# States and output products put in front of the attention scores, with a shorter opening: a one-core decoder layer on Trainium2

## The chip, the cores and the metric

The kernel runs on one core of a Trainium2 chip. The metric is the device time of one execution in microseconds (us). Before the change it was 455.96 us, the median of 3 runs (455.81 to 457.31). The profiler recorded one execution by itself, of 455.39 us; its trace spans 453.6 us, and all times of the trace count from the start of that span. The engines are called PE (matrix products), PEld (PE's weight loads), DVE (vector), ACT (scalar functions), POOL and SP; SP's work here is to issue DMA transfers.

## What is computed

One decoder layer over 512 tokens of width 1024. The input is normalised and multiplied with one wide weight matrix, whose columns are cut into branches:

```python
aq, ak, av, ag, bq, bf, bi, bg, gate_a, gate_b = jnp.split(proj, split_pts, axis=-1)
# attention branch: 8 heads of 64
qa = rmsnorm(heads(aq), q_norm_gain[i])
ka = rmsnorm(heads(ak), k_norm_gain[i])
ya = moba_attention(qa, ka, va, rel_bias)          # logits + bias, softmax, times values
ya = (ya * silu(ag)) @ w_up_a[i]
# recurrent branch: 4 heads of 128
log_f = log_sigmoid(fpre) + log1p(lb * exp(minimum(-fpre, EXP_CLIP)))
kb = (1.0 - lb) * sigmoid(-fpre);  qb = silu(bq);  vb = bi
yb = hgrn2_chunkwise(qb, kb, vb, log_f)            # chunk by chunk:
#   out   = (q * exp(cum)) @ state + scores @ v
#   state = state * exp(last) + (k * exp(last - cum)).T @ v
yb = (rmsnorm(yb, hgrn_out_gain) * silu(bg)) @ w_up_b[i]
merged = sigmoid(gate_a) * ya + sigmoid(gate_b) * yb
h = h + merged @ w_out[i];  h = h + (p @ w_ple) * sigmoid(h @ w_ple_gate)
```

All is in float32. Every large product is split into three: each operand is a rounded high half and a low half, and high·high, high·low and low·high are added up.

## The kernel before, in words

A projection is 24 products of 128x128 by 128x512: 8 slices of the inner dimension, three products each (`mm3`, L282). The weight slices come in by DMA as `wf`; ACT makes the high half `wh` (L217), DVE the low half `wl` (L218). The projections run in this order: `bi`, `av` (values), `bf0`, `bq0`, `aq`, `ak`, then the table `ORDER` (`bg0`, `ag0`, `bf1`, ...), then the up-projections, the output and the last gate. The two letters name the branch of the weight, `ga`/`gb` the merge gates, and the digit the head or the column block.

Into this stream of dense products small ones are woven. The recurrent branch works head by head (h = 0 to 3): the gates (`hgrn_gates`), the products within a chunk `lpb` and `lpa` (`hgrn_intra`, tiles of 128x32), the chunk states (`hds` products, then `st` on DVE), and the output products `hop` (`hgrn_out`). The attention branch works pair of heads by pair of heads: the scores `s` of step 0 (query blocks 0 to 2) and of step 1 (block 3), the softmax, sixteen SP transfers per step that turn the probabilities (L836), and the products with the values, `o`. `s01` is written here for head pair 0, step 1.

PE's order is fixed as the program writes it. A planner (`tick`, `run_due`, `spawn`) decides where: it adds up the expected time of the dense products, and a generator that is due puts its products there. `PACE` is the planner's time between two attention steps. The output products `hop` of a head wait in a list `hops` until the next head's `hgrn_intra` comes to `lpb`; `hds` follows `lpa` of its own head at once. The order on ACT, DVE and SP is made by a scheduler from costs and due times; `held` makes an instruction stand behind the last dense product written so far, `in_order` and `tc.high_priority` set rank.

PSUM, where the products land, is a set of banks: three for the pool `mm` (projections, `hop`, `o` and the third score tile `s{hp}0x`), two for `g` (`lpb`, `lpa`, `hds`), three for `a` (`aq`, `ak`, the other score tiles). A product that starts a new tile waits until the last reader of the bank's former tile is done. For a gate projection (`bg1`, `bg2`, ...) that reader is the DVE multiply at the end of `silu_block` (L479), behind three ACT instructions (exp, ln, exp); for a `bq` it is the multiply at L514.

At the start, nine products of ones (`warm`, L184) run on PE while the first data comes: `xhead` (L328), then the first weight's first slice in two transfers of 256 columns (L330), all on SP's queue; the small constants `smalls` come by ACT's queue (L179). `lower_bound` (L205 to L213) computes a few 128x4 constants from them.

Of the kernel before, what the change touches and what calls it, by code (L numbers as in the profile page):

```python
# [28 lines left out]
LEVELS = (16, 8, 4, 2, 1)  # L29

STEPS = ((0, 1, 2), (3,))
PACE = (21.0, 21.0)

HP = 2.5
H0 = 8.0
# [8 lines left out]

EARLY = (2, 3, 4, 5)

WARM = 9

XN = (0.6,) * 7 + (2.0, 0.6)

# [13 lines left out]
def hybrid_layer_kernel(  # L64
# [75 lines left out]

    dense = []

    def held(inst):

        tc.add_manual_dep(inst.ins, dense[-1].ins.name,
                          mybir.DependencyInfo(mybir.DependencyClass.NoSync, mybir.DependencyReason.SCHED_ONLY))
        return inst

    def held_from(us, insts, until=None):

        def later():
            for inst in insts if until not in done else []:
                held(inst)
            yield 0.0

        spawn(later(), us)
# [19 lines left out]
    raw0 = unit("w", "wf0", shape=(128, 2, 512))  # L176
    A.preload_act_table_set("natural_log_exp_and_others")
    with tc.high_priority():
        nc.scalar.dma_start(sm, smalls)  # L179

    warm = bank("g", "warm")
# [20 lines left out]
    lbv, ln1mlb = lb[:, 3], lb[:, 5]  # L202

    def lower_bound():
        V.tensor_scalar(qgain, sm[:, 8:9], 0.125, None, op0=OP.mult)  # L205
        V.tensor_copy(lb[:, 0], lbl)
        V.tensor_sub(lb[:, 1], lbl, lb[:, 0])
        A.activation(lb[:, 1], lb[:, 1], AF.Exp)
        V.reciprocal(lb[:, 2], lb[:, 1])
        V.tensor_mul(lb[:, 2], lb[:, 1], lb[:, 2])  # L210
        V.tensor_sub(lb[:, 3], lb[:, 2], lb[:, 2])
        V.tensor_scalar(lb[:, 4], lb[:, 3], -1.0, 1.0, op0=OP.mult, op1=OP.add)
        A.activation(lb[:, 5], lb[:, 4], AF.Ln)  # L213


    def split(hi, lo, src):
        A.activation(hi, src, AF.Copy)  # L217
        V.tensor_tensor(lo, src, hi.bitcast(F32), op=OP.subtract)  # L218
# [2 lines left out]
        A.activation(hi, src, AF.Copy, scale=g)  # L221
        V.scalar_tensor_tensor(lo, src, g, hi.bitcast(F32), op0=OP.mult, op1=OP.subtract)

    wseq, wraw, wtile, wpos = [], [], [], [0]
    late = []

    def w_sequence():
# [31 lines left out]
    def w_split(upto):  # L259
        while len(wtile) <= min(upto, len(wseq) - 1):  # L260
            i = len(wtile)
            w_load(i)
            ap, kn, cols = wseq[i]
            hi = unit("wh", f"wh{i}", R, (128, kn, cols))
            lo = unit("wl", f"wl{i}", R, (128, kn, cols))
            split(hi, lo, wraw[i])
            wtile.append((hi, lo))

    def weight(ap, ahead=LD):
# [56 lines left out]

    with tc.high_priority():
        nc.sync.dma_start(xfirst, xhead)  # L328
        for i in range(2):
            nc.sync.dma_start(raw0[:, 0, 256 * i:256 * i + 256], wseq[0][0][:, 0, 256 * i:256 * i + 256])  # L330
        x0 = unit("H", "xr0")
        xr.append(x0)
        nc.sync.dma_start(x0[:, 256:512], xT[0][:, 256:512])
        raw1 = unit("w", "wf1", shape=(128, 2, 512))
        wraw.append(raw1)
        nc.sync.dma_start(raw1[:, 0], wseq[1][0][:, 0])
        load_x(1, 2)
        nc.sync.dma_start(raw0[:, 1], wseq[0][0][:, 1])
        nc.sync.dma_start(raw1[:, 1], wseq[1][0][:, 1])
        load_x(2, 3)  # L340
# [141 lines left out]


    hg = {}
    hops = []

    runs = [1000]

# [28 lines left out]
    def hgrn_intra(h):  # L517
# [50 lines left out]
        k16 = kq(16)  # L568
        yield HP
        yield from beside_attention()  # L570
        while hops:
            hops.pop()()
        lpb = bank("g", f"lpb{h}").rearrange("p (l c t) -> p l c t", l=4, c=NT)
        big = lpb[:, 2:4].rearrange("p l c t -> p (l c t)").rearrange("p (c t) -> p c t", c=NT)
        lpa = bank("g", f"lpa{h}").rearrange("p (l c t) -> p l c t", l=4, c=NT)
# [50 lines left out]
        if not h:  # L626
# [4 lines left out]
        V.tensor_tensor(q[:, 128:], q[:, 128:], cum[:, 128:], op=OP.mult)  # L631
        turned = A.activation(kd[:, :nk].rearrange("p (c g k) -> p g c k", c=3, g=4),
                              kts[:, :nk].rearrange("p (g c k) -> p g c k", g=4, c=3), AF.Copy)
        held(turned) if h == 0 else held_from(2.0, [turned], f"hds{h}")
        yield from beside_attention()
        for i, k_ in enumerate(ks):
            diag(lpa[:, 1 + i], k_, k_, LEVELS[1 + i])
# [4 lines left out]
            A.activation(sc[s_, :, s_], s32[s_], AF.Copy)  # L642
        hg[h] += (kd,)

    def hgrn_out(h, vb, sbg):
        kb, q, cum, kd = hg[h][:4]
        hv = slice(h * 128, h * 128 + 128)
        dsp = bank("g", f"hds{h}")
        done.add(f"hds{h}")
        for c in range(3):  # L650
            PE.matmul(dsp[:, c * 128:c * 128 + 128], kd[:, c * 128:c * 128 + 128], vb[c][:, hv],
                      start=True, stop=True)
        cost(0.65)
        st = unit("st", f"st{h}", shape=(128, 3, 128))
        V.tensor_copy(st[:, 0], dsp[:, 0:128])
        for c in (1, 2):
            e = c * 128 + 127
            V.scalar_tensor_tensor(st[:, c], st[:, c - 1], cum[:, e:e + 1], dsp[:, c * 128:c * 128 + 128],
                                   op0=OP.mult, op1=OP.add)
        op_ = []  # L660

        def products():
            op_.append(bank("mm", f"hop{h}"))
            for c in range(NT):
                s_ = slice(c * 128, c * 128 + 128)
                PE.matmul(op_[0][:, s_], vb[c][:, hv], sc[:, c, :], start=True, stop=(c == 0))
                if c:
                    PE.matmul(op_[0][:, s_], st[:, c - 1], q[:, s_], start=False, stop=True)
            cost(1.5)

        if h < GH - 1:
            hops.append(products)
            yield lambda: op_
        else:
            yield HOP
            products()
        op_ = op_[0]
        o = unit("YB", f"ho{h}")
        y = unit("N", f"hy{h}")
        A.activation(o, op_, AF.Square)  # L680
        gated = f"bg{h}" in done
        if gated:
            V.scalar_tensor_tensor(sbg[h], op_, ogain[:, h:h + 1], sbg[h], op0=OP.mult, op1=OP.mult)
        token_spread(y, token_factor(token_sums(o, y, 1.0 / 128)))
        if gated:
            V.tensor_tensor(sbg[h], sbg[h], y, op=OP.mult)
        else:
            V.scalar_tensor_tensor(o, op_, ogain[:, h:h + 1], y, op0=OP.mult, op1=OP.mult)
        hg[h] += (None if gated else o,)
# [28 lines left out]
    def qk_norm(name, banks, g, res):  # L718
# [6 lines left out]
        for t in range(NT):  # L725
            raw = pb[:, (0 if name == "q" else 4) + t]
            with tc.high_priority(offset=AHEAD):
                A.activation(raw, banks[t], AF.Copy)
            sq = pb[:, 8 + t % 2]
            A.activation(sq, raw, AF.Square)  # L730
            V.tensor_reduce(ss[:, t], sq.rearrange("p (h d) -> p h d", h=HEADS), axis=AX.X, op=OP.add)
            raws.append(raw)
        V.tensor_scalar(ss, ss, 1.0 / 64, None, op0=OP.mult)
        rsqrt(y, t_, ss)
        for t in range(NT):
# [38 lines left out]
    def attention(qn, kn, va, sags, res):  # L774
# [92 lines left out]
        for n in range(len(steps) + 1):  # L867
            if n >= 1:
                yield PACE[steps[n - 1][1]]
            if n < len(steps):  # L870
                hp, i = steps[n]
                if i == 0:
                    for j in range(2):
                        t = unit("T", f"bias{hp}{j}")
                        row = ed[2 * hp + j:2 * hp + j + 1, :]
                        held(nc.sync.dma_start(t, bass.AP(tensor=row.tensor, offset=row.offset,
                                                          ap=[[1, 128], [1, 512]])))
                        T[hp, j] = t
                where = scores(hp, i)
            if n >= 1 and steps[n - 1][1] == NS - 1:  # L880
                ho = steps[n - 1][0]
# [256 lines left out]
```

## Time and profile before

| | before |
|---|---|
| time, median of 3 (lowest to highest) | 455.96 us (455.81 to 457.31) |
| profiled execution, its span | 455.39 us, 453.6 us |
| PE busy | 448.7 us, 99% |
| DVE, ACT busy | 303.1 us, 276.5 us |
| granted PE clock | 0.999 |
| POOL's DMA queue, SP's DMA queue, share of 16 engines | 22.7%, 20.0% |

How it is read: the timeline gives start, duration, engine, source line, operation, output <- inputs, and in brackets how long the engine sat idle before it and what ended that. A PE product's recorded duration (0.39 us for 512 columns) is longer than the distance to the next one's start (0.227 us), because products overlap; costs on PE are therefore taken from start to start. "PEld" rows are the weight loads. "issue" means that the profile shows no event that was waited for.

### The profile page before, as it was taken

How to read it: one execution, taken by the hardware profiler on the slowest of the kernel's cores; microseconds unless marked ns; L12 is line 12 of the kernel's file. 1: busy time of each engine (PE TensorE's matmuls, PEld its weight loads, DVE VectorE, ACT ScalarE, POOL GpSimd, SP SyncE). 2: the span in 40 equal slices, each digit the busy share in tenths (PEclk: the TensorE clock that was granted, in tenths of full speed). 3: DMA queues.
4: the chain of work that ended last, by engine and by line, in shares of the span. 5: the costliest groups of instructions: out<-in, count | busy, mean ns of one | idle time of the engine just before them, and what ended most of it. 6: DMA issues, size and time to landing. Idle time of an engine off the chain costs nothing.

```text
span 453.6 us, 8108 instructions
## 1 busy us (share of the span) xinstructions
PE 448.7 (99%) x3066; PEld 372.3 (82%) x3066; DVE 303.1 (67%) x616; ACT 276.5 (61%) x532; POOL 38.4 (8%) x77
## 2 busy tenths in 40 slices
PE   9999999999999999999999999999999999999996
PEld 8888888788888888878888888878888888888886
DVE  5869493876898795959985866454479744544322
ACT  5957574737679986979887987683334433222201
POOL 1000100000000000010101000101220100000000
PEclk9999999999999999999999999999999999999999
DMA  8802433258492527162526352545731644230111
GB/s 257 322 1 95 139 104 117 79 201 185 166 260 74 171 53 220 30 177 92 163 86 175 103 160 95 166 143 139 249 94 48 229 141 140 92 115 25 46 48 46
DMA packets 31846, 59.49 MB, mean 131 GB/s; under 512 B 6976, under 2 KB 16960, under 8 KB 31808
## 3 DMA queue, kind: packets, MB, share of 16 engines
q0 software_dynamic: 9056, 32.51, 22.7%
q1 hardware_dynamic: 22608, 26.47, 20.0%
q8 instruction: 24, 0.39, 0.4%
q14 instruction: 14, 0.11, 0.1%
q10 hardware_dynamic: 144, 0.01, 0.0%
HBM read 48.74 MB, written 4.98 MB: 118 GB/s over the span
## 4 chain that ended last, share of the span: by engine, by line
PE 81%; DVE 7%; SPq 4%; DMA 3%; ACT 2%; issue 2%; DVEq 0%; ACTq 0%
PE g L282 10%; PE ga L282 10%; PE h L282 10%; PE ub L282 5%; PE ua L282 5%; PE av L412 5%; PE bi L412 5%; PE aq L412 4%; SPq L836 4%; PE ak L412 4%; PE gb L282 4%; PE bf L282 4%; PE ag L282 4%; PE bg L282 3%; PE bq L282 3%; PE pe L282 2%
## 5 line engine op out<-in xcount | busy, mean ns | idle before, releaser
L217 ACT ACTIVATE wh<-wf 128x1024 fp32r<-128x1024 f32 (+1 forms) x78 | 75.6, 969 | 96.1 <-issue 32.2
L218 DVE TENSOR_TENSOR wl<-wf,wh 128x1024 fp32r<-128x1024 f32 (+1 forms) x78 | 86.6, 1111 | 56.9 <-ACT wh L217 56.5
L256 POOL DMA_DIRECT2D wf<-in_w_tr_dram x30 | 15.8, 528 | 171.1 <-DVE wl L218 109.7
L282 PE MATMUL g<-hh,wh 128*128 128x512 f32 (+1 forms) x72 | 26.3, 365 | 0.0
L282 PE MATMUL g<-hl,wh 128*128 128x512 f32 (+1 forms) x72 | 26.3, 365 | 0.0
L282 PE MATMUL g<-hh,wl 128*128 128x512 f32 (+1 forms) x72 | 26.3, 365 | 0.0
L282 PE MATMUL ga<-xh,wh 128*128 128x512 f32 x64 | 25.2, 394 | 0.0
L282 PE MATMUL gb<-xh,wh 128*128 128x512 f32 x64 | 25.0, 391 | 0.0
L282 PE MATMUL ga<-xh,wl 128*128 128x512 f32 x64 | 24.9, 390 | 0.0
L282 PE MATMUL ga<-xl,wh 128*128 128x512 f32 x64 | 24.9, 389 | 0.0
L282 PE MATMUL gb<-xl,wh 128*128 128x512 f32 x64 | 24.9, 389 | 0.0
L282 PE MATMUL h<-mh,wh 128*128 128x512 f32 x64 | 24.9, 389 | 0.0
L282 PE MATMUL h<-ml,wh 128*128 128x512 f32 x64 | 24.9, 389 | 0.0
L282 PE MATMUL h<-mh,wl 128*128 128x512 f32 x64 | 24.9, 389 | 0.0
L282 PE MATMUL gb<-xh,wl 128*128 128x512 f32 x64 | 24.9, 389 | 0.0
L820 ACT ACTIVATE pb<-pb,ps 128x128 f32<-128x128 f32 (+3 forms) x32 | 17.6, 552 | 10.4 <-DVE ps L818 10.1
L818 DVE CUSTOM_DVE_ANT_0 pb<-s,bias 128x128 f32<-128x128 f32 (+3 forms) x28 | 12.9, 498 | 8.7 <-DMA bias<-in_ed_dram 5.7
L1025 DVE TENSOR_TENSOR hf<-h,xres 128x512 f32<-128x512 f32 x8 | 5.5, 691 | 16.5 <-PE h L282 16.5
L822 ACT ACTIVATE pb<-pb,ps 128x128 f32<-128x128 f32 (+3 forms) x32 | 16.3, 550 | 0.2 <-DVE ps L821 0.2
L530 ACT ACTIVATE hx<-hx 128x512 f32<-128x512 f32 x24 | 14.8, 622 | 1.4 <-DVE hx L529 1.3
L282 PEld LDWEIGHTS g<-hl,wh 128*128 128x128 f32 x72 | 13.6, 189 | 2.2
L282 PEld LDWEIGHTS g<-hh,wh 128*128 128x128 f32 x72 | 13.6, 189 | 2.2
(346 smaller groups left out, 1245.1 us busy)
## 6 DMA issues: line engine op xcount, KB each, us to landing
wf<-in_w_tr_dram POOLq DMA_DIRECT2D x30, 512.0 KB, 4.2
wf<-in_w_tok_dram POOLq DMA_DIRECT2D x8, 512.0 KB, 3.6
wf<-in_w_up_dram POOLq DMA_DIRECT2D x16, 256.0 KB, 3.0
wf<-in_w_o_dram POOLq DMA_DIRECT2D x8, 512.0 KB, 4.4
wf<-in_w_g_dram POOLq DMA_DIRECT2D x8, 512.0 KB, 3.6
wf<-in_w_tok_dram SPq DMA_DIRECT2D x6, 512.0 KB, 6.9
pb<-pb SPq DMA_DIRECT2D x64, 48.0 KB, 3.0
bias<-in_ed_dram SPq DMA_DIRECT2D x8, 256.0 KB, 4.3
```

The source lines that it names most:

```text
L217: A.activation(hi, src, AF.Copy)
L218: V.tensor_tensor(lo, src, hi.bitcast(F32), op=OP.subtract)
L256: (G if len(wraw) >= FAR else nc.sync).dma_start(raw, ap)
L282: dense.append(PE.matmul(ps, a[:, k, :], b[k], start=(n == 0), stop=(n == tot - 1)))
L412: dense.append(PE.matmul(banks[t], a[:, s_], b[:, kk, :], start=(k == 0 and i == 0), stop=(k == KD - 1 and i == 2)))
L530: A.activation(x, x, AF.Exp)
L818: in_order(V.tensor_tensor_reduce(p_, s_[:, so:so + nk], T[j][:, nk - 1::-1], -1.0, 3e38, OP.add, OP.min, st[:, 0:1]))
L820: A.activation(p_, p_, AF.Exp, bias=st[:, 0:1], scale=-1.0, accum_out=st[:, 1:2])
L822: A.activation(p_, p_, AF.Copy, scale=st[:, 2:3])
L836: nc.sync.dma_start(pt[32 * b:32 * b + 32, a], z[32 * a:32 * a + 32, b])
L1025: V.tensor_tensor(t, ps, xres, op=OP.add)
```

## The change

```diff
-PACE = (21.0, 21.0)
+PACE = (19.5, 20.5)
-WARM = 9
+WARM = 7
+WAIT = 16
+    def behind(inst, other):
+        tc.add_manual_dep(inst.ins, other.ins.name, ...SCHED_ONLY)
+        return inst
     def held(inst):
+        return behind(inst, dense[-1])
     with tc.high_priority():
+        nc.scalar.dma_start(raw0[:, 0, 0:256], w_tok[2, 0][:, 0, 0:256])
         nc.scalar.dma_start(sm, smalls)
     def lower_bound():
-        V.tensor_scalar(qgain, sm[:, 8:9], 0.125, None, op0=OP.mult)
-        V.tensor_copy(lb[:, 0], lbl)
+        held(V.tensor_scalar(qgain, sm[:, 8:9], 0.125, None, op0=OP.mult))
+        held(V.tensor_copy(lb[:, 0], lbl))
-        for i in range(2):
-            nc.sync.dma_start(raw0[:, 0, 256 * i:256 * i + 256], wseq[0][0][:, 0, 256 * i:256 * i + 256])
+        nc.sync.dma_start(raw0[:, 0, 256:512], wseq[0][0][:, 0, 256:512])
-    hops = []
+    fronts = []
+    def full_array():
+        while fronts:
+            fronts.pop(0)()
...
-        while hops:
-            hops.pop()()
         lpb = bank("g", f"lpb{h}")...
...
-        held(turned) if h == 0 else held_from(2.0, [turned], f"hds{h}")
+        held(turned)
+        if h:
+            fronts.append(lambda: hgrn_states(h, kd, cum))
...
+    def hgrn_states(h, kd, cum):          # the hds products and st, cut out of hgrn_out
...
     def hgrn_out(h, vb, sbg):
+        if f"hds{h}" not in done:
+            hgrn_states(h, kd, cum)
+        st = sts[h]
         if h < GH - 1:
-            hops.append(products)
+            fronts.append(products)
...
     # qk_norm
-                A.activation(raw, banks[t], AF.Copy)
+                copied = A.activation(raw, banks[t], AF.Copy)
+        if name == "q":
+            behind(rounds[WAIT], copied)
...
     # attention, ahead of a step's scores
+                full_array()
                 where = scores(hp, i)
```

So: states wait for the next scores of a head pair's step 0 and stand right in front of them, output products for those of step 1 (`hop0`, whose head has no earlier place, for the first scores of all). The rounding `wh` of weight 16 (for the third `ak` slice) is put behind the last copy out of an `aq` bank. The first half slice of the first weight is issued by ACT's queue, ahead of `smalls`.

In the rows below a name's number tells one buffer from another; `x2` is a repeat. The first place is PE at the first scores (`s_...`, `s00x`) of head pair 0, before:

```order
L282 MATMUL bg_1343<-xh_428,wh_1245 128x512
L282 MATMUL bg_1343<-xl_429,wh_1245 128x512
L282 MATMUL bg_1343<-xh_428,wl_1246 128x512
L801 MATMUL s_1364<-kh_1130,qh_877 128x128
L801 MATMUL s_1365<-kh_1130,qh_877 128x128
L801 MATMUL s_1364<-kh_1130,ql_881 128x128
L801 MATMUL s_1365<-kh_1130,ql_881 128x128
L801 MATMUL s_1364<-kl_1134,qh_877 128x128
L801 MATMUL s_1365<-kl_1134,qh_877 128x128
L801 MATMUL s_1366<-kh_1130,qh_877 128x256
L801 MATMUL s00x<-kh_1130,qh_877 128x256
```

and now:

```order
L289 MATMUL bg_1341<-xh_426,wl_1244 128x512
L686 MATMUL hop_1362<-sc,biv_391 128x128 x2
L688 MATMUL hop_1362<-ha_607,st_1093 128x128
L686 MATMUL hop_1362<-sc,biv_394 128x128
L688 MATMUL hop_1362<-ha_607,st_1093 128x128
L686 MATMUL hop_1362<-sc,biv_394 128x128
L688 MATMUL hop_1362<-ha_607,st_1093 128x128
L823 MATMUL s_1370<-kh_1128,qh_875 128x128
L823 MATMUL s_1371<-kh_1128,qh_875 128x128
```

The output products of head 0 now stand between the ninth product of `bg1` and the scores. They take the bank that `bf1` leaves; `s00x`, which took that bank before, now takes the one that `bq1` leaves.

The second place is PE at the second scores of head pair 0, before:

```order
L282 MATMUL bf_1555<-xh_485,wl_1475 128x512
L282 MATMUL bq_1586<-xh_412,wh_1516 128x512
L282 MATMUL bq_1586<-xl_413,wh_1516 128x512
L282 MATMUL bq_1586<-xh_412,wl_1517 128x512
L282 MATMUL bq_1586<-xh_420,wh_1516 128x512
L282 MATMUL bq_1586<-xl_421,wh_1516 128x512
L282 MATMUL bq_1586<-xh_420,wl_1517 128x512
L801 MATMUL s_1593<-kh_1130,qh_877 128x512
L801 MATMUL s_1594<-kh_1130,qh_877 128x512
L801 MATMUL s_1593<-kh_1130,ql_881 128x512
L801 MATMUL s_1594<-kh_1130,ql_881 128x512
```

and now:

```order
L289 MATMUL bf_1594<-xh_483,wl_1514 128x512
L823 MATMUL s_1619<-kh_1128,qh_875 128x512
L823 MATMUL s_1620<-kh_1128,qh_875 128x512
L823 MATMUL s_1619<-kh_1128,ql_879 128x512
L823 MATMUL s_1620<-kh_1128,ql_879 128x512
L823 MATMUL s_1619<-kl_1132,qh_875 128x512
L823 MATMUL s_1620<-kl_1132,qh_875 128x512
L589 MATMUL lpb_1655<-hx_64_1346 32x64 x8
```

The scores now follow the last product of `bf2`, without the six products of `bq2`; behind them `lpb` follows directly, where `hop` stood. The same pattern recurs for pairs 1 and 2, with three products of `bq3` and six of `gb6` ahead of `hop` and the scores; `hds`, which followed `lpa`, stands ahead of `s10`, `s20` and `s30`.

The third place is ACT where it finishes the gate `bg2` (`bg2s`: L287 exp, L288 ln, L289 exp; in the changed kernel these lines are L294 to L296), before:

```order
L217 ACTIVATE wh_2096<-wf_2094 128x1024
L287 ACTIVATE bg2s<-bg_1889 128x512
L288 ACTIVATE bg2s<-bg2s,onec 128x512
L289 ACTIVATE bg2s<-bg2s 128x512
L217 ACTIVATE wh_2143<-wf_2141 128x1024
L287 ACTIVATE ag2s<-ag_2100 128x512
L642 ACTIVATE sc<-s_1347 32x4x32 x4
```

and now:

```order
L272 ACTIVATE wh_2087<-wf_2085 128x1024
L294 ACTIVATE bg2s<-bg_1887 128x512
L653 ACTIVATE sc<-s_1345 32x4x32 x4
L295 ACTIVATE bg2s<-bg2s,onec 128x512
L272 ACTIVATE wh_2136<-wf_2134 128x1024
L294 ACTIVATE ag2s<-ag_2091 128x512
L296 ACTIVATE bg2s<-bg2s 128x512
```

The second exp of `bg2s` now stands behind the four copies `sc<-s`, the next `wh` and the first exp of `ag2s`. For `bg3s` the order changes in the same way. On DVE the multiply that ends `bg2s` stood between two `wl` (L218); now it stands behind both.

More of the change, by code (lines that the diff above doesn't have):

```diff
@@ L141, in hybrid_layer_kernel, with held @@
     dense = []
-    def held(inst):
-        tc.add_manual_dep(inst.ins, dense[-1].ins.name,
+    def behind(inst, other):
+        tc.add_manual_dep(inst.ins, other.ins.name,
                           mybir.DependencyInfo(mybir.DependencyClass.NoSync, mybir.DependencyReason.SCHED_ONLY))
         return inst
+    def held(inst):
+        return behind(inst, dense[-1])
     def held_from(us, insts, until=None):
@@ L222, in scale_split @@
         V.scalar_tensor_tensor(lo, src, g, hi.bitcast(F32), op0=OP.mult, op1=OP.subtract)
-    wseq, wraw, wtile, wpos = [], [], [], [0]
+    wseq, wraw, wtile, wpos, rounds = [], [], [], [0], {}
     late = []
@@ L265, in w_split @@
             lo = unit("wl", f"wl{i}", R, (128, kn, cols))
-            split(hi, lo, wraw[i])
+            rounds[i] = A.activation(hi, wraw[i], AF.Copy)
+            V.tensor_tensor(lo, wraw[i], hi.bitcast(F32), op=OP.subtract)
             wtile.append((hi, lo))
@@ L643, in hgrn_intra @@
         hg[h] += (kd,)
-    def hgrn_out(h, vb, sbg):
-        kb, q, cum, kd = hg[h][:4]
+    sts = {}
+    def hgrn_states(h, kd, cum):
         hv = slice(h * 128, h * 128 + 128)
@@ L659, in hgrn_out @@
                                    op0=OP.mult, op1=OP.add)
+        sts[h] = st
+    def hgrn_out(h, vb, sbg):
+        kb, q, cum, kd = hg[h][:4]
+        hv = slice(h * 128, h * 128 + 128)
+        if f"hds{h}" not in done:
+            hgrn_states(h, kd, cum)
+        st = sts[h]
         op_ = []
```

## The prediction

> **What bounds the kernel now.** I read the page's head, then the waits of PE and of its weight loads, then PE's timeline from start to start.
>
> ```profile
> span 453.6 us, 8108 instructions
> PE 448.7 (99%) x3066; PEld 372.3 (82%) x3066; DVE 303.1 (67%) x616; ACT 276.5 (61%) x532; POOL 38.4 (8%) x77
> ...
> PE ak L412 <- ACT pb L728: 0.3, 1, 0.3
> ...
> PEld bf L282 <- DVE bg2s L479: 0.3, 1, 0.3
> ```
>
> PE is busy 99% of the span, so what counts is the number of PE's slots, the few gaps, and whatever new gap comes in. Only one wait of a product is recorded in the stream (`ak` on ACT). The `bf` row is short, but it says that PE reaches `bf3` just as a DVE multiply frees its PSUM bank: there is no slack there. My sum is made against the profiled execution (span 453.6, time 455.39) and then carried to the median, 455.96, which is 0.57 above it. About 0.3% (1.4 us) is what a measurement can tell from no change.
>
> **The opening** (seven warming products, first half slice by ACT's queue).
>
> ```profile
> 0.78 4.18 PE L184 MATMUL warm<-const-float32-1.0 128*128 128x128 f32 x18 [0.78 <-PEq L1126]
> 4.61 0.74 PE L443 MATMUL bi<-wh,gh 128*128 128x256 f32 x2
> 5.18 0.40 PE L443 MATMUL bi<-wh,gl 128*128 128x256 f32 x2
> 6.38 0.40 PE L412 MATMUL bi<-wh,gh 128*128 128x512 f32 x1
> ...
> 1.18 0.89 SPq L330 DMA_DIRECT2D wf<-in_w_tok_dram  x2
> ...
> 3.59 0.29 DVE L363 CAST wh<-wf 128x256 fp32r<-128x256 f32 x1
> ```
>
> The nine warming products (recorded as 18 rows) take 4.61 - 0.78 = 3.83 us, 0.43 each; seven end at about 3.8. The data are ready at 3.59 + 0.29 = 3.88, and the half slice is now issued at about 0.73, not 1.18. So the first pair could start at 3.8 to 4.0. The first pair takes 0.57 us (4.61 to 5.18), the five behind it (6.38 - 5.18) / 5 = 0.24 each: the clock rises at about 5.0. If it still does, two pairs run slowly (4.0 to 5.1) and four at 0.24, to 6.0 instead of 6.38. SP's later first loads each move up by one issue (0.45), so the next slices follow. I take a gain of 0.45; bounds: 0.85 (two warming products whole) and a loss of 0.5 (inputs half a microsecond later, or the clock rising later).
>
> The Trainium skill speaks against the second queue: "DMA: Bandwidth & Descriptors", section "Rules for kernel authors", says that spreading DMAs over engines doesn't help, since all use the same 16 DMA engines, and only saves issue time. By that the earlier slice would delay `xhead`, and the gain would be near nothing; no row here shows the two in flight together from two queues.
>
> `lower_bound`'s nine small operations leave the opening for a place near 46 us, where DVE idles:
>
> ```profile
> 3.32 0.16 DVE L206 COPY lb<-sm 128x4 f32<-128x4 f32 x1
> ...
> 48.32 1.23 DVE L218 TENSOR_TENSOR wl<-wf,wh 128x1024 fp32r<-128x1024 f32 x1 [2.32 <-ACT wh L217]
> ```
>
> Nine times about 0.16 is 1.5 us, under 2.32 of idle time: nothing. Without that cover the `wl` would come at most 1 us later.
>
> **The `ak` gap** (round 16 behind the last `aq` copy).
>
> ```profile
> 85.66 1.05 ACT L217 ACTIVATE wh<-wf 128x1024 fp32r<-128x1024 f32 x1
> 86.73 0.60 ACT L728 ACTIVATE pb<-aq 128x512 f32<-128x512 f32 x1
> ...
> 86.69 0.39 PE L412 MATMUL ak<-wl,xh 128*128 128x512 f32 x1
> 87.38 0.50 PE L412 MATMUL ak<-wh,xh 128*128 128x512 f32 x1 [0.31 <-ACT pb L728]
> ```
>
> From 86.69 to 87.38 is 0.69, where 0.227 is normal, and the restart costs another 0.1 (as below at a change of shape): 0.56 lost while PE waits for the bank that the copy empties. With the copy first it ends at 85.66 + 0.60 = 86.26; PE arrives at 86.92. Gain 0.55. The weight that now comes 0.6 later is used only for the third `ak` slice; bounds 0.3 to 0.6.
>
> **Fewer changes of array shape.**
>
> ```profile
> 154.22 0.50 PE L801 MATMUL s<-kh,qh 64*128 64x512 f32 x2
> 154.55 0.40 PE L801 MATMUL s<-kh,ql 64*128 64x512 f32 x2
> 154.79 0.40 PE L801 MATMUL s<-kl,qh 64*128 64x512 f32 x2
> 155.11 0.71 PE L666 MATMUL hop<-sc,biv 128*128 128x128 f32 x4
> 155.66 0.39 PE L668 MATMUL hop<-ha,st 128*128 128x128 f32 x2
> ...
> 156.87 0.43 PE L580 MATMUL lpb<-hx 128*32 128x64 f32 x16
> ```
>
> Where the tile shape changes, PE loses time on both sides: 0.33 instead of 0.24 at the start of `s` (154.22 to 154.55), 0.32 instead of 0.24 before `hop` (154.79 to 155.11), 0.55 instead of 0.44 at `hop`'s start: about 0.2 per change. `hop` (128*128 like the dense products) now stands before `s` rather than between `s` and `lpb`: one change less for each of three heads, 0.6; bounds 0.3 and 0.8. `hds` moves with the same number of changes. The gains add up to 0.45 + 0.55 + 0.6 = 1.6.
>
> **New wait 1, `s00x`.**
>
> ```profile
> 131.80 0.33 PE L801 MATMUL s00x<-kh,qh 64*128 64x256 f32 x1
> ...
> 133.40 0.68 DVE L514 TENSOR_TENSOR ha<-ha,bq 128x512 f32<-128x512 f32 x1
> ```
>
> `s00x` now takes the bank of `bq1`, free when this multiply ends, at 134.08. `hop` (155.11 to 156.87, 1.76, less 0.2 of shape changes) moves `s00x` from 131.80 to 133.36. PE waits 0.72 and restarts: 0.8. Queued behind it are all PE's products. Bounds 0 and 0.9.
>
> **New wait 2, `bf3`.** It takes the bank of `bg2`.
>
> ```profile
> 152.54 0.39 PE L282 MATMUL bf<-xh,wl 128*128 128x512 f32 x1
> 176.94 0.33 PE L801 MATMUL s<-kh,qh 64*128 64x128 f32 x2
> 195.39 0.50 PE L282 MATMUL bf<-xh,wh 128*128 128x512 f32 x1
> ...
> 153.83 1.23 DVE L218 TENSOR_TENSOR wl<-wf,wh 128x1024 fp32r<-128x1024 f32 x1 [1.62 <-ACT wh L217]
> 155.22 0.69 DVE L818 CUSTOM_DVE_ANT_0 pb<-s,bias 128x512 f32<-128x512 f32 x1 [0.16 <-PE s L801]
> 164.96 0.70 DVE L825 STREAM_TRANSPOSE pb<-pb 128x512 f32<-128x512 f32 x1
> 181.33 0.29 DVE L818 CUSTOM_DVE_ANT_0 pb<-s,bias 128x128 f32<-128x128 f32 x1 [4.13 <-DMA bias<-in_ed_dram]
> 194.65 0.68 DVE L479 TENSOR_TENSOR bg2s<-bg2s,bg 128x512 f32<-128x512 f32 x1
> ...
> 192.42 0.63 ACT L289 ACTIVATE bg2s<-bg2s 128x512 f32<-128x512 f32 x1
> 192.96 1.04 ACT L217 ACTIVATE wh<-wf 128x1024 fp32r<-128x1024 f32 x1
> 194.38 1.25 ACT L642 ACTIVATE sc<-s 32x128 f32<-32x128 f32 x4
> ```
>
> Four steps. (a) *Arrival.* PE went from `s10` to `bf3` in 195.39 - 176.94 = 18.45; without `hds` (0.69, next to `s10` on its other side now) it is 17.76. (b) *Bias.* DVE idles 4.13 until SP's bias transfer lands at 181.33, `s10` + 4.39; SP issues it behind the sixteen transfers that the transpose at 164.96 (end 165.66, `s01` + 11.4) releases. Now `s01` stands right behind `bf2`, and DVE's `wl` before the first bias add can't start until `bf2` ends (as at 153.83, 1 us after it): the first add comes 2.1 after `s01`, not 1.0, so the transpose ends at `s01` + 12.5 to 12.9. From `s01` to `s10` it is 22.72 before; less `hop` 1.76, plus six products 1.36, plus `hds` 0.69: 23.0. The 15.67 from transposes to bias stay, or shrink to 14.1, as for the next pair (213.31 below). So the bias lands at `s10` + 3.6 to 5.5. (c) *Release.* Before, the multiply ended at 195.33, bias + 14.0, and ACT's last exp had ended 1.6 before it began. The four copies, a `wh` and another exp now stand ahead of that exp: 1.25 + 0.95 + 0.55 = 2.75, less 1.6 of slack: bias + 15.15; 15.7 if the copies wait for DVE. (d) *The wait*: 3.6 + 15.05 - 17.76 = 0.9 to 5.5 + 15.7 - 17.76 = 3.4. I take 2.0.
>
> **New wait 3, `ga1`**, which takes the bank of `bg3`.
>
> ```profile
> 213.31 0.70 DVE L825 STREAM_TRANSPOSE pb<-pb 128x512 f32<-128x512 f32 x1
> 228.11 0.29 DVE L818 CUSTOM_DVE_ANT_0 pb<-s,bias 128x128 f32<-128x128 f32 x1 [0.88 <-DMA bias<-in_ed_dram]
> 241.17 0.67 DVE L479 TENSOR_TENSOR bg3s<-bg3s,bg 128x512 f32<-128x512 f32 x1
> ...
> 225.01 0.33 PE L801 MATMUL s<-kh,qh 64*128 64x128 f32 x2
> 243.77 0.39 PE L282 MATMUL ga<-xh,wh 128*128 128x512 f32 x1
> ```
>
> Arrival was 18.76 after `s20`; without `hds` 0.69 and with three `bg3` products (0.68) gone ahead of `s20`, 17.4, or 17.1 if the 0.3 us that `o1` lost goes too. The bias comes at `s20` + 3.1, the multiply ended 13.7 after it; the same three ACT items put in front make it 15.0. The wait is 18.1 - 17.2 = 0.9; bounds 0 and 1.4.
>
> Sum: 0.8 + 2.0 + 0.9 - 1.6 = +2.1, so 457.5 for a profiled execution and 458.1 for the median.
>
> **The rivals.** *The multiplies keep up.* If the removed `st` work (it moves into DVE's 4.13 us of idle time) brings ACT and DVE forward by as much as the new order costs, none of the three waits shows and the gains stay: 455.96 - 1.6 = 454.4. For it: DVE idles a third of the time. Against it: the zero slack at `bf3`, and ACT's order is written in the build. *A part of the waits binds*, say `s00x` and half of `bf3`: 0.8 + 1.0 - 1.6 = +0.2, 456.2. *The bias is late* (slower than the forecast): both `bf3` at 3.4 and `ga1` at 1.4 with 0.8 give 5.6 - 1.6 = +4.0, 460.0; it decides from a bias landing 5 us after `s10`. *The opening gives nothing*, since the two transfers share the DMA engines: +0.45 on each case; its place would be a later end of the cast at 3.59.
>
> The clock is a fourth unknown: the Trainium skill, "TensorE: Matmul & The Clock Gate", Part 1, has half rate for some 3.4 us of a free-running window, so that the rise would wander by half a microsecond between runs. By that the opening would be worth 0.2 to 0.7, and nothing else changes; one profiled execution can't show it.
>
> **How the numbers follow.** Three waits near my values: 0.40, with a range of its own of 457.2 to 459.2. Late bias: 0.10. A part of the waits: 0.28. None: 0.22. The first two are slower by over 0.3% (0.50), the third within it, the fourth faster. The range that leaves out a tenth on each side runs from 454.3 to 459.7.
>
> **What would show it.** In the changed profile: waits of `s` on a multiply of `ha,bq` (0.7), of `bf` on `bg2s` (2) and of `ga` on `bg3s` (0.9); the first `bi` near 4.0; no wait of `ak`; `s` to `lpb` without `hop`. The forecast is wrong if the bias lands less than 3 us after `s10`, or if ACT's last exp of `bg2s` ends within 13 us of it.

## The result, and the profile after

The changed kernel takes 461.0 us (median of 6 runs, 460.26 to 463.31); the kernel before, run beside it, 456.16. The ratio is 1.0106, 95% interval 1.0084 to 1.0129. The forecast of 458.1 had the right side and the wrong size: 461.0 lies above its range, 454.3 to 459.7. The profiled execution took 460.53 us with a span of 458.8, against 455.39 and 453.6: +5.2 to explain.

The head of the page, after the change:

```profile
span 458.8 us, 8088 instructions
PE 448.8 (98%) x3062; PEld 372.3 (81%) x3062; DVE 303.7 (66%) x616; ACT 275.4 (60%) x532; POOL 38.5 (8%) x77
```

PE works as long as before (448.8 against 448.7), so the 5.2 us are gaps. The waits of PE, after (columns: engine, line, what was waited for; us in total, times, longest):

```profile
PE ga L289 <- DVE bg3s L485: 2.0, 1, 2.0
PE o L871 <- DMA bias<-in_ed_dram: 1.6, 2, 1.0
...
PE bf L289 <- DVE bg2s L485: 0.8, 1, 0.8
PE bi L449 <- ACT gh L227: 0.5, 1, 0.5
PE s00x L823 <- DVE ha L525: 0.4, 1, 0.4
```

The forecast named `ga`, `bf` and `s00x`; it didn't name `o`, nor the first `bi`. The row of `ak` is gone. PE's timeline at these places:

```profile
4.55 0.77 PE L449 MATMUL bi<-wh,gh 128*128 128x256 f32 x2 [0.45 <-ACT gh L227]
...
133.52 0.38 PE L823 MATMUL s00x<-kh,qh 64*128 64x256 f32 x1 [0.44 <-DVE ha L525]
...
154.65 0.50 PE L823 MATMUL s<-kh,qh 64*128 64x512 f32 x2
...
177.65 0.33 PE L823 MATMUL s<-kh,qh 64*128 64x128 f32 x2
...
181.57 1.09 PE L871 MATMUL o<-pb,avv 128*64 128x128 f32 x16 [0.98 <-DMA bias<-in_ed_dram]
...
197.53 0.50 PE L289 MATMUL bf<-xh,wh 128*128 128x512 f32 x1 [0.77 <-DVE bg2s L485]
...
205.46 0.50 PE L823 MATMUL s<-kh,qh 64*128 64x512 f32 x2
...
228.37 0.33 PE L823 MATMUL s<-kh,qh 64*128 64x128 f32 x2
...
231.94 1.09 PE L871 MATMUL o<-pb,avv 128*64 128x128 f32 x16 [0.61 <-DMA bias<-in_ed_dram]
...
235.71 0.50 PE L289 MATMUL ag<-xh,wh 128*128 128x512 f32 x1
...
248.94 0.50 PE L289 MATMUL ga<-xh,wh 128*128 128x512 f32 x1 [2.03 <-DVE bg3s L485]
```

From start to start on PE in the two traces (us), the 5.2 divide like this:

| place | before | after | change | forecast |
|---|---|---|---|---|
| opening: first `bi`; first full `bi` product | 4.61; 6.38 | 4.55; 6.37 | 0 | -0.45 |
| `ak` | 17.70 | 17.09 | -0.61 | -0.55 |
| `s00`, where `s00x` waits | 1.41 | 2.24 | +0.83 | +0.8 |
| pair 1: `o0`, then `gb` up to `bf3` | 2.33, 5.45 | 3.53, 6.37 | +1.20, +0.92 | +2.0, all at `bf3` |
| pair 2: `o1`; from the last `bg3` product to `ag3` | 2.65; 0.23 | 3.16; 0.50 | +0.51; +0.27 | not named |
| pair 2: `ag3`; first `ga` group | 5.44; 10.88 | 5.59; 13.21 | +0.15; +2.33 | +0.9, all at `ga` |
| `bf2` up to what follows it | 5.53 | 5.64 | +0.11 | not named |
| what is left over: shape changes | | | -0.53 | -0.6 |

The changes add up to 5.2. The forecast's terms add up to 2.1: of the 3.1 us that are missing, 2.4 are at pair 2, 0.45 in the opening, and the rest in pieces of 0.1 at the other places.

**Pair 2.** The timelines of DVE and SP, after:

```profile
208.36 0.65 DVE L840 CUSTOM_DVE_ANT_0 pb<-s,bias 128x512 f32<-128x512 f32 x1
...
212.08 0.67 DVE L311 TENSOR_REDUCE npart<-hy 128x16 f32<-128x512 f32 x1
...
217.13 0.69 DVE L847 STREAM_TRANSPOSE pb<-pb 128x512 f32<-128x512 f32 x1
...
228.69 0.57 DVE L619 STREAM_TRANSPOSE hkt<-hkd 128x384 f32<-128x384 f32 x1
...
233.97 0.29 DVE L840 CUSTOM_DVE_ANT_0 pb<-s,bias 128x128 f32<-128x128 f32 x1 [4.10 <-DMA bias<-in_ed_dram]
...
235.24 0.41 DVE L840 CUSTOM_DVE_ANT_0 pb<-s20x,bias 128x256 f32<-128x256 f32 x1
...
248.20 0.68 DVE L485 TENSOR_TENSOR bg3s<-bg3s,bg 128x512 f32<-128x512 f32 x1
...
228.65 1.06 SPq L898 DMA_DIRECT2D bias<-in_ed_dram  x2
229.81 0.38 SPq L622 DMA_DIRECT2D hkt3there<-hkt  x1
```

and DVE before, right behind the last transpose:

```profile
213.94 0.64 DVE L304 TENSOR_REDUCE npart<-hy 128x16 f32<-128x512 f32 x1
```

The first bias add comes at 233.97, `s20` + 5.6, where the forecast carried over the + 3.1 of before. The last transpose of the step before ends at 217.82, `s11` + 12.4 (before: 214.00, + 11.6): 0.8 later. The second bias add comes 2.9 after `s11`, much as before (3.0): two DVE operations on the output products' result (`bg1s` and `hy`, 207.07 to 208.36, 1.3 us) now stand ahead of it, but a `wl` (1.2) that stood ahead of both adds before is already done. The delay arises from that add to the last transpose: `npart`, a third operation on that result (0.6), and four more `hx` operations of the recurrent head (0.33 each) now stand there, where they stood behind it before, and only the 1.3 us are gone from there. SP issues its sixteen transfers and comes to the bias row 10.8 later (before 10.1): 0.7. From the issue to the add it takes 5.3 (before 4.0): 1.3. From `s11` to `s20` PE takes 0.3 longer than before (22.9, before 22.6), which makes the add that much less late. Together: 0.8 + 0.7 + 1.3 - 0.3 = 2.5 us. The release is as forecast: `bg3s` ends at 248.88, 14.9 after the add. The wait ahead of `ag3` is the late bias as well: the add that reads the score tile `s20x` ends at 235.65, and `ag3` starts at 235.71. The profile counts it among the waits of PE's weight loads (0.5), so it isn't in the list above.

What follows the bias on SP's queue is new, and might explain the 1.3. `hkt3there`, one transfer of 192 KB, was issued at 235.20 before, behind the bias adds; now the transpose that releases it (228.69) stands ahead of them on DVE, and it starts 1.2 us behind the bias row. The transfers of 226 to 236 us, after (KB each, median us from issue to landing):

```profile
bias<-in_ed_dram SPq DMA_DIRECT2D x2, 256.0 KB, 5.2
hkt3there<-hkt SPq DMA_DIRECT2D x1, 192.0 KB, 5.2
```

and those of 221 to 231 us before:

```profile
bias<-in_ed_dram SPq DMA_DIRECT2D x2, 256.0 KB, 3.9
```

The wait of `o` has to do with the sixteen transfers, which are its input. Of 228.0 to 228.6 us, after, the last of them:

```profile
pb<-pb SPq DMA_DIRECT2D x1, 32.0 KB, 3.5
```

It is issued just ahead of the bias row, at 228.02, and lands 3.5 later, at 231.5; the second half of `o1` starts at 231.94. The profile puts that wait down to the bias, but the bias lands only about 233.8, just before its add, so it can't be that.

**The opening.** ACT's row of the first `gh`, before:

```profile
3.08 0.51 ACT L221 ACTIVATE gh<-pb 128x256 fp32r<-128x256 f32 x1 [0.62 <-DMA pb<-in_xhead_dram]
```

and ACT and DVE after:

```profile
3.91 0.51 ACT L227 ACTIVATE gh<-pb 128x256 fp32r<-128x256 f32 x1 [0.97 <-DMA pb<-in_xhead_dram]
...
4.12 0.29 DVE L369 CAST wh<-wf 128x256 fp32r<-128x256 f32 x1 [3.21 <-DMA wf<-in_w_tok_dram]
```

`xhead`, issued when it always was, lands 0.8 later, and the half slice, issued 0.45 earlier, 0.5 later. The Trainium skill, "DMA: Bandwidth & Descriptors", section "Rules for kernel authors", says that spreading transfers over engines brings no bandwidth. This trace agrees, with 3.08 to 3.91 as its price.

### The profile page after: what moved, and what is told of

The parts are those of the page before. It is cut to its first block, busy times and chain, and to the rows that moved or that the text cites. A ratio compares the mean times of both kernels' runs of the same rounds, so it can differ in the third digit from the quotient of the medians.

```text
span 458.8 us, 8088 instructions
## 1 busy us (share of the span) xinstructions
PE 448.8 (98%) x3062; PEld 372.3 (81%) x3062; DVE 303.7 (66%) x616; ACT 275.4 (60%) x532; POOL 38.5 (8%) x77
## 4 chain that ended last, share of the span: by engine, by line
PE 73%; ACT 12%; DVE 6%; SPq 4%; DMA 3%; issue 1%; DVEq 0%; ACTq 0%
PE g L289 10%; PE h L289 9%; PE ga L289 8%; PE ub L289 5%; PE aq L418 5%; PE ak L418 5%; PE ua L289 5%; PE av L418 5%; PE bi L418 4%; SPq L858 4%; PE bf L289 4%; PE gb L289 2%; PE pe L289 2%; ACT wh L272 2%; DMA bias<-in_ed_dram 2%; ACT pb L844 2%
## 5 line engine op out<-in xcount | busy, mean ns | idle before, releaser
L262 POOL DMA_DIRECT2D wf<-in_w_tr_dram x30 | 15.9, 529 | 176.5 <-DVE wl L273 162.7
L289 PE MATMUL ga<-xh,wh 128*128 128x512 f32 x64 | 25.4, 396 | 2.0 <-DVE bg3s L485 2.0
L289 PE MATMUL g<-hh,wh 128*128 128x512 f32 (+1 forms) x72 | 26.3, 365 | 0.0
L289 PE MATMUL g<-hl,wh 128*128 128x512 f32 (+1 forms) x72 | 26.3, 365 | 0.0
L289 PE MATMUL g<-hh,wl 128*128 128x512 f32 (+1 forms) x72 | 26.3, 365 | 0.0
L289 PE MATMUL gb<-xh,wh 128*128 128x512 f32 x64 | 25.0, 391 | 0.0
L289 PE MATMUL ga<-xh,wl 128*128 128x512 f32 x64 | 24.9, 390 | 0.0
L289 PE MATMUL ga<-xl,wh 128*128 128x512 f32 x64 | 24.9, 390 | 0.0
L289 PE MATMUL gb<-xl,wh 128*128 128x512 f32 x64 | 24.9, 389 | 0.0
L289 PE MATMUL h<-mh,wh 128*128 128x512 f32 x64 | 24.9, 389 | 0.0
L289 PE MATMUL h<-ml,wh 128*128 128x512 f32 x64 | 24.9, 389 | 0.0
L289 PE MATMUL h<-mh,wl 128*128 128x512 f32 x64 | 24.9, 389 | 0.0
L289 PE MATMUL gb<-xh,wl 128*128 128x512 f32 x64 | 24.9, 389 | 0.0
L840 DVE CUSTOM_DVE_ANT_0 pb<-s,bias 128x128 f32<-128x128 f32 (+3 forms) x28 | 13.0, 495 | 11.6 <-DMA bias<-in_ed_dram 10.2
L289 PEld LDWEIGHTS ga<-xh,wh 128*128 128x128 f32 x64 | 12.0, 188 | 5.3 <-DVE bg3s L485 2.5
L289 PEld LDWEIGHTS g<-hh,wh 128*128 128x128 f32 x72 | 13.6, 189 | 2.2
```

Of the source, the lines that this page charges most:

```text
L262: (G if len(wraw) >= FAR else nc.sync).dma_start(raw, ap)
L289: dense.append(PE.matmul(ps, a[:, k, :], b[k], start=(n == 0), stop=(n == tot - 1)))
L840: in_order(V.tensor_tensor_reduce(p_, s_[:, so:so + nk], T[j][:, nk - 1::-1], -1.0, 3e38, OP.add, OP.min, st[:, 0:1]))
```

## Experiments: the opening and the `ak` gap

Each is the kernel before with one part of the change. The first has the whole opening: seven warming products, the first half slice by ACT's queue, `lower_bound` held back.

```diff
-WARM = 9
+WARM = 7
+        nc.scalar.dma_start(raw0[:, 0, 0:256], w_tok[2, 0][:, 0, 0:256])
-        for i in range(2):
-            nc.sync.dma_start(raw0[:, 0, 256 * i:256 * i + 256], ...)
+        nc.sync.dma_start(raw0[:, 0, 256:512], wseq[0][0][:, 0, 256:512])
+        held(...)    # the operations of lower_bound
```

> The kernel before with the opening of the change alone (seven warming products, first half slice by ACT's queue, lower_bound held back). The prediction's own step: first product at about 4.0 us instead of 4.61 and a gain of 0.4 to 0.5 us. Rival (the two transfers share the DMA engines): gh is ready about 0.8 us later, the first product again comes near 4.55, and the gain is 0.0 to 0.1.

456.84 us, ratio 1.0012 [0.9992, 1.0032]: no change. The inputs are late here too (the cast starts at 3.91), in the timeline of ACT of this run:

```profile
3.72 0.51 ACT L222 ACTIVATE gh<-pb 128x256 fp32r<-128x256 f32 x1 [0.78 <-DMA pb<-in_xhead_dram]
```

The second leaves the half slice on SP's queue, and keeps the seven products and the held `lower_bound`.

```diff
-WARM = 9
+WARM = 7
+        held(...)    # the operations of lower_bound
```

> As the first run, but the first weight is loaded as before, by SP's queue alone. If sharing is what makes gh late, gh is ready at 3.6 and the cast at 3.9 as before, the first product comes at about 3.9 and the gain is 0.3 to 0.6 us. If the inputs are late for another reason, the first product again comes near 4.5.

456.47 us, ratio 1.0002 [0.9988, 1.0017]. `gh` starts at 3.00, the first `bi` at 3.98 and the full products at 5.82 instead of 6.38. Then the weight loads of `av` wait, by the waits of this run (and as long once more for ACT's half of the same slice):

```profile
PEld av L412 <- DVE wl L371: 0.4, 1, 0.4
```

and the second group of `bi` products starts at 10.47, where it started at 10.48 before. The gain that was expected (0.3 to 0.6) doesn't come: an earlier start is worth nothing by itself, as the next weight slice's landing is the next bound.

The third has the changed wait of weight 16 alone.

```diff
+        if name == "q":
+            behind(rounds[WAIT], copied)
```

> The kernel before with only the rounding of weight 16 put behind the last aq copy. The wait of ak goes: 0.55 us faster, first bg at 106.4 instead of 107.0. Rival: another wait takes its place and the first bg stays at 107.0.

455.99 us, ratio 0.9984 [0.9967, 1.0000]. `ak` takes 17.10, so the 0.6 us are there in the trace; the times alone would hardly show them, and its span is 453.6 us all the same, as the opening ran slower in this execution.

## Experiments: which link of the bias chain

The theory: from the scores of one step hang, in one chain, the softmax, its transposes, sixteen transfers, the next pair's bias row, its adds on DVE, and at the end the multiply that frees a bank for `bf3` or `ga`. The chain got longer on its own side and its distance on PE shorter. If so, issuing the bias rows a step earlier, ahead of the sixteen transfers, takes both waits away.

```diff
-                if i == 0:
-                    for j in range(2): ...          # bias of pair hp
+                if n == 0:
+                    load_bias(0)
+                if i == 1 and hp + 1 < HPAIRS:
+                    load_bias(hp + 1)
```

> The changed kernel with the next pair's bias rows issued one attention step earlier, between the two groups of sixteen transfers instead of behind both. Theory 1 (the late bias makes the releases late): DVE's first add comes within 0.7 us of s10 and s20, the multiplies of bg2s and bg3s end 15 us after it, the waits of bf3 (0.9) and ga1 (2.3) and of ag3 go, those of s00x (0.8) and o0 (1.2) stay: about 3.5 us faster than the changed kernel, 457 to 458. Theory 2 (the order on ACT alone): the waits of bf3 and ga1 stay and the time is 460 to 461.

456.9 us, ratio to the kernel before 1.0009 [0.9990, 1.0028]; span 455.0 against 458.8 with all else as changed. The waits of PE in this run:

```profile
PE o L871 <- DMA hkt3there<-hkt: 0.8, 1, 0.8
...
PE o L871 <- DMA hkt2there<-hkt: 0.7, 1, 0.7
```

`bf3` and `ga` wait no more (`gb` 5.44, `ga` 10.88). `o0` and `o1` still take 3.28 and 3.39, `s00` 2.23. So the bias row's lateness is worth 3.8 us of the 5.2.

Is it the shorter pace? First the changed kernel with the old one, then the kernel before with the new one.

```diff
-PACE = (19.5, 20.5)
+PACE = (21.0, 21.0)
```

> The changed kernel with PACE back at (21, 21) and nothing else undone. Theory 1 (the shorter pace puts the second scores right behind bf2 and bf3, which makes the bias and the probabilities late): bg2 and bg3 are done ahead of s10 and s20, the waits of o0 (1.2), bf3 (0.9), o1 (0.8) and ga1 (2.3) go, that of s00x (0.8) stays: 455.5 to 456.5. Theory 2 (states and output products in front make them late, whatever the pace): the waits stay and the time is 460 to 461.

462.29 us, ratio 1.0123 [1.0097, 1.0150]. Pair 1 is free (`o0` 2.33, `gb` 5.44), but PE waits in other places, at `o1` and much later at `ub`:

```profile
PE o L871 <- DVE bg3s L485: 2.7, 1, 2.7
PE ub L289 <- ACT ybh L223: 1.8, 1, 1.8
```

and the granted clock falls behind both. Stretches of this run (us, PE busy, granted clock, DMA share, GB/s):

```profile
230.00:234.50 4.50, 2.31 (x25) 1.00 0.44 135
234.50:239.00 4.50, 4.02 (x43) 0.62 0.60 180
...
313.00:317.00 4.00, 3.87 (x12) 0.60 0.11 27
```

With 0.62 and 0.60 granted on the mean, these two stretches of 4.5 and 4.0 us lose 1.7 and 1.6 us beside the waits.

```diff
-PACE = (21.0, 21.0)
+PACE = (19.5, 20.5)
```

> The kernel before with PACE (19.5, 20.5) alone, states and output products where they were. Theory 1: the second scores again stand right behind bf2, the bias lands late, and PE waits 2 to 5 us in all for probabilities and for the banks of bg2 and bg3: 458 to 461. Theory 2: no new waits, 456.

456.69 us, ratio 1.0006 [0.9990, 1.0021]. The new pace alone costs next to nothing, and taking it back from the changed kernel helps nothing: the pace is not the cause. It is the products and states ahead of the scores that cost, with either pace, and the pace decides at which waits.

The release: the copies `sc` stood behind the last exponential of the gate before, and stand ahead of it now. Put behind it again:

```diff
         sigmoid(t, ps)
+        if name in ("bg2", "bg3"):
+            for c in copies[int(name[2]) - 1]:
+                behind(c, last[0])          # last[0]: the exponential that ends sigmoid
```

> The changed kernel, with the four copies sc<-s put behind the last exp of bg2s and of bg3s as they were before the change; the bias stays late. By the prediction's release term the multiply of bg2s ends 14.0 after the bias instead of 14.9 and the wait of bf3 (0.9) goes; that of bg3s ends 1.2 earlier and the wait of ga1 falls from 2.3 to 1.1: 2 us faster, 459. If the lateness is the bias alone, the gain is under 0.5 us.

459.24 us, ratio 1.0062 [1.0045, 1.0078]: 1.8 below the changed kernel. The waits of PE:

```profile
PE o L878 <- DMA bias<-in_ed_dram: 2.4, 2, 1.7
...
PE ga L289 <- DVE bg3s L492: 0.4, 1, 0.4
```

From bias add to the end of the multiply it is 12.6 (`bg2s`) and 13.7 us (`bg3s`), where the changed kernel has 14.9. `bf3` doesn't wait, `ga` hardly.

Then three edits together: the early bias rows, the old pace, and nothing in front of the very first scores.

```diff
+                if i == 1 and hp + 1 < HPAIRS:
+                    load_bias(hp + 1)
-PACE = (19.5, 20.5)
+PACE = (21.0, 21.0)
-                full_array()
+                if n:
+                    full_array()
```

> The changed kernel with the bias rows issued one attention step earlier, PACE (21, 21), and the first output product in front of the second scores instead of the first. All new waits should be gone: s00x, o0, o1, bf3 and ga1. Against the kernel before, the ak wait (0.6) and some shape changes (0.3 to 0.6) are saved: 455.0 to 455.6. If one wait stays (o0 at 1 us), 456 to 457.

461.9 us, ratio 1.0117 [1.0092, 1.0141], a miss: the waits of `o` on `bg3s` (2.2 us) and of `ub` on `ybh` (1.8) are those of the run with the old pace. With that pace it is not the bias that holds `o1`: its rows are early here, and the wait is there all the same.

## Experiments: the collision, the states, and what remains

Behind the bias adds again, as before the change: the transpose of the last head's keys, which releases `hkt3there`.

```diff
+            if h == 3:
+                behind(turning, adds[h - 1])    # turning: the transpose of hkt; adds: last bias add of a pair's first scores
```

> The changed kernel, with one thing more: VectorE's transpose of the last head's keys (hkt3) stays behind the six bias adds of pair 2's first scores, as it stood before the change, so that the five transfers that it releases are issued later. It also puts the copies of the diagonal blocks (sc) behind the exponentials of bg3s on ScalarE. Theory 'the transfers collide': pair 2's bias row took 5.3 us from its issue to its add in the changed kernel and 4.0 before, because hkt3's transfers were issued right behind it; with those gone it is back at 4.0 us, and bg3s ends at least 1.3 us earlier (up to 2 with the sc copies behind it), so ga comes down from 13.2 us to 11.9 or less, at best 10.9; the whole 1.3 to 2.3 us faster than the changed kernel: 458.7 to 459.7. Rival 'the split's weight tile and the write of the sorted groups make the row late, not hkt3': the row still takes 5.3 us from its issue, ga gains only what the sc copies cost (0.6 at most), and the whole is within 0.6 us of the changed kernel's 461.0.

459.67 us, ratio 1.0072 [1.0050, 1.0094]. The transfers of 226 to 236 us:

```profile
bias<-in_ed_dram SPq DMA_DIRECT2D x2, 256.0 KB, 4.2
```

The row lands 4.2 instead of 5.2 us after its issue. `ga` comes down from 13.21 to 12.00, 0.1 above what the theory asked for, and the median by 1.3, though the intervals of the two ratios overlap. That the transfer beside the row was the cause isn't shown. In the run with the copies `sc` put behind, `hkt3there` follows the row just as closely (issued at 229.24, the row at 228.09), and in pair 1 of the changed kernel `hkt2there` does, with 192 KB too (179.19 and 178.04). The transfers of 226 to 233 us in the former, and of 176.5 to 183 us in the latter:

```profile
bias<-in_ed_dram SPq DMA_DIRECT2D x2, 256.0 KB, 4.5
```

```profile
bias<-in_ed_dram SPq DMA_DIRECT2D x2, 256.0 KB, 4.4
```

In the kernel before, pair 1's row took 4.6 with no such transfer behind it. Up to pair 2 this kernel has the changed kernel's order, yet `o0` took 4.02 instead of 3.53 here: so much moves between two executions.

The changed kernel with its states back behind `lpa`:

```diff
-        if h:
-            fronts.append(lambda: hgrn_states(h, kd, cum))
```

> The changed kernel with its chunk states (hds1 to hds3) put back where they stood, behind the last of a head's diagonal products; the output products, the pace, the opening and the wait for weight 16 stay as changed. Theory 'it is the states': without the three products of hds ahead of the scores (0.69 us) and with hkt's transposes and sc's copies again behind the bias adds and the exponentials, the bias of pair 2 lands about 4 us after its issue, the waits of bf3 and ga nearly go (gb 5.4 to 5.7, ga 10.9 to 11.4), and the whole loses 2.5 to 3.3 of its 5: about 457.7 to 458.5. Rival 'it is the output products and the pace': the waits of gb and ga stay above 0.7 and 1.5 us and the whole stays within 1 us of 461.0. In both, the wait of s00x (0.8 us) stays, since it hangs on the output products alone.

459.69 us, ratio 1.0076 [1.0051, 1.0100]: neither expectation. The waits of `bf3` and `ga` go, as the first had it (`gb` 5.44, `ga` 10.88), but the wait turns up at `o0` and `o1` (4.73 and 4.32):

```profile
PE o L869 <- DMA pb<-pb: 2.2, 1, 2.2
PE o L869 <- DMA bias<-in_ed_dram: 1.8, 1, 1.8
```

The reason is in the chain. The transposes are as late (`s01` + 13.2, `s11` + 12.4), and without `hds` ahead of them `s10` and `s20`, and `o` behind each, come 0.7 sooner after `s01` and `s11`; so `o`, which needs the last of the sixteen transfers, meets the lateness first, and nothing is left of it for `bf3` and `ga`. This order of events is read in the trace and wasn't tried by itself. And again a gap of 2.2 us costs clock, in the stretches of this run:

```profile
179.00:183.00 4.00, 1.82 (x30) 1.00 0.86 238
184.35:187.70 3.35, 3.35 (x85) 0.50 0.03 7
```

Then the early bias rows, and nothing in front of the first scores, at the new pace:

```diff
+                if i == 1 and hp + 1 < HPAIRS:
+                    load_bias(hp + 1)
-                full_array()
+                if n:
+                    full_array()
```

> The changed kernel with the next pair's bias rows issued a step earlier (as in the run with the early bias, 456.9) and, as a second edit, with nothing put in front of the very first scores, so that the output product of head 0 stands behind them. Theory 'the terms add up': the 0.8 us of s00x goes as well, the waits of o0 and o1 (about 1.0 each) stay, and the whole is 455.9 to 456.3, the time of the kernel before. Rival 'the first scores' wait is only moved': the output product behind the scores makes a later step late by as much (bf1 or bg1), and the whole stays at 456.7 to 457.1.

456.26 us, ratio 0.9999 [0.9983, 1.0015]. `s00` is back at 1.41 and no later step waits for it. PE's waits that are left:

```profile
PE o L871 <- DMA hkt2there<-hkt: 0.8, 1, 0.8
...
PE o L871 <- DMA hkt3there<-hkt: 0.3, 1, 0.3
```

The change's cost is gone, and with it the gain: what `ak` and the shape changes bring, 0.6 and some 0.5 us, `o0` and `o1` take back (3.34 and 2.91 us against 2.33 and 2.65, 1.3 together).

Last, the kernel before with the two edits that the runs speak for, the wait of weight 16 and the early bias rows:

```diff
+        if name == "q":
+            behind(rounds[WAIT], copied)
+                if i == 1 and hp + 1 < HPAIRS:
+                    load_bias(hp + 1)
```

> The kernel before, with two edits: the rounding of weight tile 16 waits for the copies out of aq (which took 0.6 us off ak in the run with that edit alone) and the next pair's bias rows are issued a step earlier. Theory 'the bias is late in the kernel before too': there s20's chain ends about 0.3 us before it is needed, so early rows gain nothing on TensorE's path and only the 0.6 us of ak remains: 455.4 to 456.0 where the kernel before has 456.2 to 456.6. Rival 'the early rows collide with the sixteen transfers of the step before': o0 and o1 wait 0.5 to 1.0 us each, as in the changed kernel with early rows, and the time is 456.5 to 458.

454.56 us (454.48 to 455.54), ratio 0.9962 [0.9947, 0.9977]: faster than both kernels, and a little more than expected. The one wait that PE's list still has is the start-up of the warming products.

Against the trace of before, `ak` gives 0.61, `o1` 0.32 (2.65 to 2.33) and `bf3` 0.15 (5.59 to 5.44). Of these 1.1 us the spans show 0.5 (453.6 and 453.1), since the slow products of the opening went on for longer in this execution (first full `bi` product at 6.91 instead of 6.38). What the early bias rows bring by themselves to the kernel before wasn't tried: the interval of the run with the wait alone (0.9967 to 1.0000) overlaps this one, and there, with the bias rows as before, `o1` took 2.33 too.

## Why the prediction was wrong, step by step

- **The `bf3` term (2.0)** held in its size, not in its place. Transposes at `s01` + 12.7 (forecast 12.5 to 12.9), bias at `s10` + 4.9 (3.6 to 5.5), release 14.9 (15.05): 4.9 + 14.9 - 17.76 = 2.0, and PE lost 2.1. (Step (c) came to 15.15, and step (d) went on with 15.05; the 0.1 changes nothing.) But 1.2 of it was lost at `o0`: the sixteen transfers that make the bias late are `o`'s own input, and the step followed them to the bias alone.
- **The `ga1` term (0.9)** is the step that failed. Its release (15.0) held at 14.9; its bias at `s20` + 3.1 was carried over from the trace of before, although step (b) had just shown for pair 1 how work on DVE delays the transposes, and with them the row. With the 5.6 that was measured the same sum gives 5.6 + 14.9 - 17.2 = 3.3, and `o1`, the start of `ag3`, `ag3` and `ga` lost 3.3 together. That the late row is what makes `bf3` and `ga` wait is shown by the run with the early bias rows, where they don't. Why it was 2.5 later is known in part: 0.8 is DVE work that now stands ahead of the transposes (`npart` and four of `hx`; read in the trace, not tried). Why SP's issuing of the sixteen took 10.8 instead of 10.1, and why the row then took 5.3 instead of 4.0, stays open; the transfer of `hkt3` beside the row may have a part in it, but other rows with such a neighbour landed in 4.4 and 4.5.
- **The opening (gain of 0.45)** failed twice: the rival in which the second queue brings nothing was right, as the inputs come late with it and on time without it, and the run without the second queue shows that even a start 0.56 earlier is stopped by the next weight slice. The 0.45 wasn't the prediction's own sum either: two slow pairs of 0.57 from 4.0 on and four of 0.24 end at 6.1, not 6.0, which is 0.3 ahead of 6.38.
- **The `ak` term** (0.55; measured 0.61) and **`s00x`** (0.8; 0.83) held. **Shape changes** (0.6) held too as far as is known: 0.53 is left over for them.
- **Of the rivals** the late bias was right in mechanism: it was to decide from a landing at `s10` + 5, and the adds came at `s10` + 4.9 and `s20` + 5.6. Its 460.0 lacks the opening's 0.45, and with that it is near 461.0; it had a chance of 0.10. That the sum is near is partly luck: it put 3.4 at `bf3` and 1.4 at `ga1`, where the trace has 2.1 and 3.3. "A part of the waits binds" (456.2) fell, as all three waits showed. "The multiplies keep up" fell: no gate's multiply came sooner on DVE's freed time.
- **The clock** did wander, further than half a microsecond. The run of the `ak` wait alone has the opening of before, and yet its first `bi` products of 256 columns keep the slow distance of 0.43 up to 6.46, where before it was 0.24 from 5.18 on; from the first `bi` to `av` it took 4.20 us instead of 3.15:

```profile
6.03 0.63 PE L449 MATMUL bi<-wh,gl 128*128 128x256 f32 x2
6.46 0.76 PE L449 MATMUL bi<-wl,gh 128*128 128x256 f32 x4
```

  The Trainium skill, "TensorE: Matmul & The Clock Gate", Part 1, puts such a wander, of half a microsecond either way, down to a free-running window. These rows show the wander, and a larger one; its reason they don't show.

## What to carry to other kernels

When a chain grows on one side (softmax, transposes, transfers, bias) and its distance on PE shrinks, apply the new offset at every place that hangs on it, at each repetition, and to the first consumer: here `o`, ahead of the bank that was being watched. If a load needs nothing of the queue it stands in, move the load out before moving products: that took 3.8 us off the changed kernel's span, and together with the wait of weight 16 it made the kernel before 0.4% faster.

## What the runs showed of the hardware

A short gap can cost clock as well. After PE gaps of 2.2 us (states back; three edits together), 2.7 us (old pace), and 1.8 with 0.2 behind it (both runs with the old pace and the output products in front), the granted clock fell to 0.50 for some 3.4 us, as in the stretch of 184.35 to 187.70 us above, so that 1.7 us more were lost behind each; the 0.62 and 0.60 of the run with the old pace are means over longer stretches. After the gap of 2.0 us at `ga` in the changed kernel it stayed at 1.00, as it did after 1.8 us at `o1` with the states back:

```profile
245.50:249.00 3.50, 1.47 (x8) 1.00 0.71 209
249.00:252.00 3.00, 3.00 (x13) 1.00 0.79 239
```

These rows are of one execution. The two slowest of the changed kernel's six, 462.15 and 463.31 us, show a mean clock of 0.994 and 0.996, and one such time at half clock would make 0.996 of 459 us: there the clock seems to have fallen.

The Trainium skill, "TensorE: Matmul & The Clock Gate", section "Why this matters for your kernels", warns of idle gaps above about 3 us. Here 2.2, and 1.8 and 0.2, were enough, so the measurement decides. Since 2.0 did no harm in the trace, the length alone doesn't settle it; what else does wasn't tried.

The 256 KB bias row, issued behind the sixteen transfers, took 3.9 to 5.2 us from its issue to its landing in the rows shown. With 192 KB issued 1.2 us behind it these are 4.4, 4.5 and 5.2, without 3.9, 4.2 and 4.6: a neighbour may slow it, but these rows don't settle that.
